# A's results beside B's merge, the weights' pool open over the stages, sums of h in three places, later tiles in the pools of h and T

## The chip, the cores and the metric

The kernel runs on 1 core of one Trainium2 chip. The metric is the device time of one execution in microseconds, as the median of several runs. In the profile PE is the matrix engine (PEld its weight loads), DVE the vector engine, ACT the scalar engine, POOL the GpSimd engine; SP does nothing here but issue DMAs, and its row in the trace is its queue, in which DMAs are issued strictly one after another.

## The reference, cut to what matters

One layer over 1024 tokens of width 1024, all in float32. `h` is the modulated RMSNorm of `x`; one projection of `h` gives the columns of three branches (A attention, B short gated convolution, C conformer convolution) and of three gates.

```python
z = h @ w_in                                   # 1024 x 8704 columns
ya = neighbourhood_attention(q, k, v, kc, vc, rpb) * silu(z[..., A_Z:B_B])
yb = bg * dw_conv(cg * val, w_conv) * silu(gz)
yc = silu(layer_norm(dw_conv(a * sigmoid(g), w31) + b)) * silu(z[..., C_Z:GATES])
ga, gb, gc = split(sigmoid(z[..., GATES:]), 3)
m = ga * (ya @ w_out_a) + gb * (yb @ w_out_b) + gc * (yc @ w_out_c)
out = x + gate * (m @ w_o)
```

## The kernel before

Everything lies transposed: 128 channels on the partitions, tokens along the row. A 128x512 tile is one half of the 1024 tokens of 128 channels. Float32 products are made of three matmuls of the faster fp32r kind: an operand is split into a high part (an ACT cast, `wh`, `ysh`, `lnh`) and a low part (the rest, a subtraction on DVE or POOL, `wl`, `ysl`, `lnl`), and hi x hi, hi x lo and lo x hi are added up in a PSUM bank. `split` and `wsplit` do that.

The stages, with their times in the profiled execution:

1. To 120 us: the modulation of x, its normalisation into `ha0` to `ha7` (high) and `hb0` to `hb7` (low, the list `hlf`), and the first projections.
2. 120 to 565 us: attention of four head pairs (`attend(hp)`), beside it the projections of the next pair (`qkv`, `glu`) and, at the end, eight plain projections (`plain`) that go to memory as `zad` and `zbd`. The results of attention go to memory as `yad`. `plain(6)` and `plain(7)` of the gates are issued behind the last attention's matmuls (`zaps`, `flt`).
3. 570 to 943 us: the other columns in groups of two column tiles (`group`, run through `b_start`, `b_end`, `gate_pair`, and the last two as `last_two`). A group uses seven products instead of eight blocks, with sums of blocks of `h` (tiles `T1` to `T3`, and `T4`) and of weights (`s1` to `s4`). The sums of `h` are made by `h_sums(j)`, j = 0 to 3, on POOL during stage 2 (eight instructions `hsum` each), stored in memory as `td`, and read back by `load_t`. The convolution C runs beside the groups on DVE (`conv_step`). `a_result(i, b)` multiplies A's result by its gate path on POOL (`yain`), splits it (`ysh` on ACT, `ysl` on POOL) and stores both parts in `ysd[1]`; B's results go to `ysd[0]`. Gates go to memory as `gd`.
4. 943 us to the end: three merges, each over 8 column tiles `dm` and two halves `b`, 12 matmuls each (`ops`): B first, then A, then C; the layer norm of C (`norm_steps`) advances beside B and A by a fixed number of steps per half: column sums by matmul (`sums`), the reciprocal root (`rsqrt_mean` on POOL, `diag` on DVE), its spread over the partitions (`rstd`), and the normalised and gated result (`zcin`, `ych`). A merge's PSUM halves are multiplied by the gate (`gs`, loaded from `gd`) on DVE and added into `mt`. At the end, a product with `w_o` (`fin`).

The order in which each engine works is set by the program order and a scheduler that plans it beforehand; on the chip every engine takes its list strictly in order. Between stages 3 and 4 all pools are closed and new ones opened, so a tile of stage 4 waits for the last user of the memory that it lies on.

Of the kernel before, what the change touches and what calls it, by code (L numbers as in the profile page):

```python
# [8 lines left out]
F32 = mybir.dt.float32  # L9
# [33 lines left out]
def tile_hybrid(ctx: ExitStack, tc, x, xT, cx, cond, crow, ng, w_ada, b_ada, wqkv, wz,  # L43
# [5 lines left out]
    hctx = ExitStack()  # L49
    hp_pool = hctx.enter_context(tc.tile_pool(name="hT", bufs=1))  # L50
# [68 lines left out]
    ysd = [[[dram.tile([P, S], F32, name=f"ysd{n}{i}{h}") for h in range(2)] for i in range(4)] for n in range(2)]  # L119
# [10 lines left out]
    def qkv(hp, w=None, cts=None, first=(), psc=None, mid=None):  # L130
# [41 lines left out]
        def context():  # L172
            vc = [a1.tile([P, 2, P], F32R, tag=f"vc{h}", name="vc") for h in range(2)]
# [64 lines left out]
    A_t = cst.tile([P, KT, 2], F32, name="A_t")  # L238
    B_t = cst.tile([P, KT, 2], F32, name="B_t")
# [224 lines left out]
    with tc.tile_pool(name="at", bufs=1, reuse_waits="tile") as at, \  # L464
# [45 lines left out]
        def attend(hp):  # L510
            ya = at.tile([P, 16, 64], F32, tag="ya", name="ya", bufs=1)
            for h in range(2):
# [9 lines left out]
                for cb in range(4):  # L522
# [54 lines left out]
                    dve.tensor_tensor(out=ya[hs, :, cb * 16 : cb * 16 + 16],  # L577
# [36 lines left out]
        for hp in range(4):  # L614
            attend(hp)
            if hp < 3:
                qkv(hp + 1, w1 if hp == 0 else None)
            h_sums(hp)
            if hp < 3:
                glu(hp + 1)  # L620
        for i in range(4):
            plain(ZA + i, zad[i])
# [4 lines left out]

    sctx = ExitStack()
# [22 lines left out]
    T = [[pair(sp.tile([P, 2, 512], F32R, name=f"T{i}_{j}")) for j in range(4)] for i in (1, 2, 3)]  # L651
    T4 = [pair(hlf[1][j]) for j in range(4)]

    def load_t(blocks, i):
        for j in range(4):
            t = s512("traw", "hs", 4)
            nc.sync.dma_start(t, td[i][j])
            split(*blocks[j], t, dve)

    with tc.issue_after(state["py"].ins):  # L660
        for i in (6, 7):
            plain(GT + 2 * KT + i, gd[2 * KT + i], True)
    for i in (1, 0, 2):
        load_t(T[i], i)
    load_t(T4, 3)
# [3 lines left out]
    wq = gctx.enter_context(tc.tile_pool(name="wq", bufs=1, side="right", reuse_waits="tile"))  # L669
# [56 lines left out]
    def group(ct0, ct1, use0, use1, few=pool):  # L726

        raw = []
        for ct in (ct0, ct1):
            r = wq.tile([P, D], F32, tag="wr", name="wr", bufs=3)  # L730
# [34 lines left out]

    def last_two(cts, uses):
# [24 lines left out]
        for n in two:  # L791
# [4 lines left out]
            dve.tensor_tensor(out=x[n], in0=f, in1=x[n], op=ALU.add)  # L796
        s3 = [s_(n, raw[n][0], raw[n][2], ALU.subtract, "s3") for n in two]
# [7 lines left out]
        for n in two:  # L805
# [5 lines left out]
            uses[n][1](0, y[n])  # L811
        s4 = [s_(n, raw[n][1], s2[n], ALU.subtract, "s4") for n in two]
        for n in two:
# [40 lines left out]
    def spill_split(t, n, i, b, eng):  # L854
# [3 lines left out]
        for h, o in enumerate((hi, lo)):  # L858
            nc.sync.dma_start(ysd[n][i][h][:, B512[b]], o.bitcast(F32))

# [341 lines left out]
```

## Time and profile before

| | |
|---|---|
| median of 3 runs | 1205.05 us (1199.15 to 1205.64) |
| the profiled execution | 1200.33 us, of which the span is 1198.5 us |
| mean granted clock of PE in it | 0.964 |
| PE busy | 1126.9 us (94%) |
| DVE, POOL, ACT busy | 850.8, 663.4 and 560.8 us |
| DMA | 167.87 MB, mean 140 GB/s |

All rows of the trace are of the profiled execution, and its 1200.33 us is 4.7 us under the median. A row of the timeline gives start, duration, engine, line, operation, the tile written and the tiles read, and in brackets how long the engine had been idle before it and what released it. A row of the windows gives, per stretch of time, each engine's busy time with its count of instructions, the granted clock of PE (1.00 is full), the share of DMA and the rate. A row of the chains of waits gives the waiting instruction, what released it, the total, the count and the longest.

### The profile page before, as it was taken

What the parts mean: (1) busy time and instruction counts of PE and PEld (TensorE: products, weight loads), DVE (VectorE), ACT (ScalarE), POOL (GpSimd) and SP (SyncE); (2) the same over time, 40 slices, a digit from 0 to 9 for tenths busy, and PEclk for the clock granted to TensorE, in tenths of its full rate; (3) what the DMA queues carried; (4) which work ended last, traced back from release to release, by engine and by line L of the source; (5) the groups of instructions that cost most, each with busy time, mean ns of one, the idle gap of its engine ahead of it and who ended that gap; (6) DMA issues with size and microseconds to landing.
All of it is one profiled execution on the core that took longest, in us unless ns stands there. A gap on an engine that the chain in (4) does not pass through costs nothing.

```text
span 1198.5 us, 16663 instructions
## 1 busy us (share of the span) xinstructions
PE 1126.9 (94%) x5566; PEld 961.0 (80%) x5566; DVE 850.8 (71%) x1495; ACT 560.8 (47%) x1167; POOL 663.4 (55%) x623
## 2 busy tenths in 40 slices
PE   5779699999999999998999999999999798999998
PEld 4678699899899788886788888887877476888887
DVE  7995768788877875657993897896993356679311
ACT  5575358557656688784333332324334335313110
POOL 6675845645745833310887677868888006851110
PEclk7789899999999999999899999999999798999999
DMA  9235242332322313117234434345653694662621
GB/s 354 106 136 180 72 126 84 104 108 85 111 64 77 118 63 121 56 42 236 93 102 142 124 105 149 101 154 173 190 192 132 242 406 153 205 241 88 237 80 53
DMA packets 88151, 167.87 MB, mean 140 GB/s; under 512 B 11008, under 2 KB 39424, under 8 KB 88064
## 3 DMA queue, kind: packets, MB, share of 16 engines
q1 hardware_dynamic: 83456, 164.70, 40.9%
q10 hardware_dynamic: 4608, 2.10, 0.6%
q8 instruction: 44, 0.72, 0.3%
q14 instruction: 43, 0.35, 0.1%
HBM read 120.62 MB, written 46.14 MB: 139 GB/s over the span
## 4 chain that ended last, share of the span: by engine, by line
PE 59%; DVE 17%; DMA 8%; POOL 7%; issue 4%; ACT 3%; SPq 1%; POOLq 0%; DVEq 0%; ACTq 0%
DVE cv L690 4%; PE ops L107 4%; PE ops L109 4%; PE ops L108 4%; PE pp L564 3%; PE zaps L108 3%; PE zaps L107 3%; PE zaps L109 3%; PE ps L109 3%; PE ps L107 3%; PE ps L108 3%; PE fin L109 2%; PE fin L107 2%; PE fin L108 2%; DMA wada<-in_w_ada 2%
## 5 line engine op out<-in xcount | busy, mean ns | idle before, releaser
L90 POOL TENSOR_TENSOR wl<-wr,wh 128x384 fp32r<-128x384 f32 (+2 forms) x93 | 89.6, 969 | 182.2 <-ACT wh L88 156.1
L690 DVE SCALAR_TENSOR_TENSOR cv<-upad,cf_t,cv 128x512 f32<-128x512 f32 x240 | 166.9, 747 | 0.2
L88 ACT CAST wh<-wr 128x384 fp32r<-128x384 f32 (+2 forms) x138 | 61.2, 456 | 113.5 <-DMA wr<-in_wout 46.9
L533 POOL TENSOR_TENSOR bias<-mka,vimg 128x288 f32<-128x288 bf16 (+1 forms) x64 | 59.5, 931 | 87.8 <-DVE mn L547 76.5
L639 POOL TENSOR_TENSOR wl<-s,wh 128x512 fp32r<-128x512 f32 x57 | 79.5, 1409 | 11.1 <-ACT wh L638 6.4
L638 ACT CAST wh<-s 128x512 fp32r<-128x512 f32 x76 | 46.1, 616 | 75.6 <-POOL s L642 64.1
L639 POOL TENSOR_TENSOR wl<-wr,wh 128x512 fp32r<-128x512 f32 x46 | 64.4, 1402 | 22.7 <-ACT wh L638 22.7
L569 DVE TENSOR_TENSOR plo<-pp,ph 128x512 fp32r<-128x512 f32 (+1 forms) x96 | 60.8, 640 | 8.5 <-ACT ph L567 8.0
L714 PE MATMUL ga<-ha,wh 128*128 128x512 f32 x152 | 60.6, 398 | 6.5 <-ACT wh L638 4.7
L564 PE MATMUL pp<-ident,pbuf 128*128 128x128 f32 x352 | 59.1, 273 | 1.6 <-DVE pbuf L553 1.3
L716 PE MATMUL ga<-ha,wl 128*128 128x512 f32 x152 | 60.3, 397 | 0.2 <-POOL wl L639 0.2
L715 PE MATMUL ga<-ha,wh 128*128 128x512 f32 x152 | 60.2, 396 | 0.0
L567 ACT CAST ph<-pp 128x512 fp32r<-128x512 f32 (+1 forms) x96 | 51.7, 547 | 16.8 <-PE pp L564 16.0
L549 ACT ACTIVATE pbuf<-sc,mn 128x256 f32<-128x256 f32 x64 | 30.4, 475 | 60.1 <-DVE mn L547 59.6
L1116 DVE SCALAR_TENSOR_TENSOR o<-fin,gate,xr 128x512 f32<-128x512 f32 x16 | 12.0, 751 | 59.7 <-PE fin L109 59.7
L551 DVE TENSOR_TENSOR mn<-mn 128x1 f32<-128x1 f32 x64 | 17.6, 275 | 47.0 <-ACT pbuf L550 46.7
L109 PE MATMUL fin<-mh,wl 128*128 128x512 f32 x128 | 49.8, 389 | 0.0
L108 PE MATMUL fin<-ml,wh 128*128 128x512 f32 x128 | 49.8, 389 | 0.0
L107 PE MATMUL fin<-mh,wh 128*128 128x512 f32 x128 | 49.7, 389 | 0.0
L564 PEld LDWEIGHTS pp<-ident,pbuf 128*128 128x128 f32 x352 | 42.7, 140 | 7.0 <-DVE pbuf L553 2.6
L90 DVE TENSOR_TENSOR wl<-wr,wh 128x384 fp32r<-128x384 f32 (+2 forms) x45 | 31.6, 705 | 13.9 <-ACT wh L88 13.9
L79 POOL TENSOR_TENSOR ssh<-ssh,half_neg 128x4 f32<-128x4 f32 (+1 forms) x40 | 39.4, 987 | 2.7
(382 smaller groups left out, 3970.3 us busy)
## 6 DMA issues: line engine op xcount, KB each, us to landing
wr<-in_wz SPq DMA_DIRECT2D x36, 512.0 KB, 3.9
gs<-gd SPq DMA_DIRECT2D x24, 512.0 KB, 5.2
wada<-in_w_ada SPq DMA_DIRECT2D x16, 512.0 KB, 8.7
wr<-in_wz SPq DMA_DIRECT2D x36, 192.0 KB, 2.5
cht<-chd SPq DMA_DIRECT2D x24, 256.0 KB, 3.1
gd<-gate SPq DMA_DIRECT2D x22, 256.0 KB, 3.1
vimg<-in_rpbs SPq DMA_DIRECT2D x16, 288.0 KB, 3.0
gd<-c SPq DMA_DIRECT2D x18, 256.0 KB, 3.1
```

The costliest lines, as they stand in the source:

```text
L88: act.copy(hi[:, :n], raw[:, :n])
L90: state["lo"] = lo_eng.tensor_tensor(out=lo[:, :n], in0=raw[:, :n], in1=hi[:, :n].bitcast(F32), op=ALU.subtract)
L107: pe.matmul(ps, ah, bh, start=i == 0, stop=False)
L108: pe.matmul(ps, ah, bl, start=False, stop=False)
L109: pe.matmul(ps, al, bh, start=False, stop=i == n - 1)
L564: pe.transpose(out=pp[:, c * 256 + hf * P : c * 256 + hf * P + P], in_=pts[hf][:, o : o + P], identity=ident)
L569: dve.tensor_tensor(out=plo[:, : m * 256], in0=pp[:, : m * 256], in1=ph[:, : m * 256].bitcast(F32), op=ALU.subtract)
L639: eng.tensor_tensor(out=lo, in0=src, in1=hi.bitcast(F32), op=ALU.subtract)
L690: dve.scalar_tensor_tensor(out=acc[b], in0=src, scalar=cf_t[:, i, j : j + 1], in1=acc[b], op0=ALU.mult, op1=ALU.add)
L714: pe.matmul(ps, wh, bh, start=first and j == 0, stop=False, skip_group_check=True)
L715: pe.matmul(ps, wh, bl, start=False, stop=False, skip_group_check=True)
L716: pe.matmul(ps, wl, bh, start=False, stop=last and j == 3, skip_group_check=True)
```

## The change

Six things are done.

- `h_sums` is called nowhere after the first head pair, with j = 0 after the second, j = 1 after the third, and with 2 and 3 after the fourth.
- The pool of `h` stays open to the end, with waits by tile; `T1` to `T3` lie in a pool `tp` of their own that also stays open. `load_t` loads a sum straight into the place of the low part and splits it there; T1 to T3 are loaded ahead of `plain(6)` and `plain(7)`, T4 behind the first group. A dummy tile fixes where the first tile `cht` lies.
- The first group loads its weights into two tiles of the pool `sp` (`wry`), because the pool of weights is not yet open.
- `a_result` leaves the groups. Beside B's merge, A's results and their gate paths are loaded as whole 128x1024 tiles (`a_load`), multiplied on POOL (`yz`) and split in place (`ya`), with no way through memory.
- The weights' pool `wq` stays open, so the merges load their weights in pairs (`w_raw`, `wro`) and split them 512 wide; the first two pairs, B's results (`yb`), and C's convolution (`cvin`) are loaded and prepared during `last_two`, into the tiles of T and `h` that are no longer read. The last product's weights go the same way (`wrf`).
- `norm_steps` begins two tiles of B's merge later and takes three steps per half beside B and two beside A; `rstd` is 2 matmuls of 512 columns instead of 8 of 128; `big` has 8 buffers instead of 10.

On POOL, at the start of attention (in these rows `hsum` is a sum of h, `vc`, `vs` and `ssh` belong to the context's and the latents' keys and values, `bias` to the first scores). Before:

```order
L598 TENSOR_TENSOR hsum_2457<-ha0_175 128x512
L598 TENSOR_TENSOR hsum_2459<-hb0_463 128x512
L598 TENSOR_TENSOR hsum_2463<-hb4_682 128x512
L200 TENSOR_TENSOR vc_1228<-rawc_1280,vc_1228 128x64
L200 TENSOR_TENSOR vc_1229<-rawc_1280,vc_1229 128x64
L598 TENSOR_TENSOR hsum_2469<-ha4_179 128x512
L200 TENSOR_TENSOR vc_1228<-rawc_1295,vc_1228 128x64
L533 TENSOR_TENSOR bias_1415<-mka_1366,vimg_1411 128x288
L200 TENSOR_TENSOR vc_1229<-rawc_1295,vc_1229 128x64
L533 TENSOR_TENSOR bias_1432<-mka_1366,vimg_1413 128x288
L533 TENSOR_TENSOR bias_1488<-mka_1366,vimg_1411 128x384
```

After:

```order
L202 TENSOR_TENSOR vc_1221<-rawc_1273,vc_1221 128x64
L202 TENSOR_TENSOR vc_1222<-rawc_1273,vc_1222 128x64
L202 TENSOR_TENSOR vc_1221<-rawc_1288,vc_1221 128x64
L536 TENSOR_TENSOR bias_1408<-mka_1359,vimg_1404 128x288
L202 TENSOR_TENSOR vc_1222<-rawc_1288,vc_1222 128x64
L536 TENSOR_TENSOR bias_1425<-mka_1359,vimg_1406 128x288
L536 TENSOR_TENSOR bias_1481<-mka_1359,vimg_1404 128x384
L77 TENSOR_SCALAR ssh_1277<-ssh_1277 128x2
L510 TENSOR_TENSOR vs_1394<-vb_1303,vs_1394 128x8x64
L510 TENSOR_TENSOR vs_1711<-vb_1303,vs_1711 128x8x64
```

The sums of h are gone from between the key's and the bias's instructions. On ACT, from the loads of T to the first group's weights (`wh` of `wr` or `wry`; `s` are the group's sums of weights). Before:

```order
L638 CAST T3_0_6434<-traw_6618 128x512
L638 CAST T3_1_6435<-traw_6622 128x512
L638 CAST T3_2_6436<-traw_6626 128x512
L638 CAST T3_3_6437<-traw_6630 128x512
L589 ACTIVATE flt_6583<-zaps_6558 128x512
L638 CAST hb0_463<-traw_6634 128x512
L638 CAST hb1_517<-traw_6638 128x512
L638 CAST wh_6674<-wr_6665 128x512
L638 CAST hb2_571<-traw_6642 128x512
L638 CAST hb3_625<-traw_6646 128x512
L638 CAST wh_6695<-s2_6670 128x512
```

After:

```order
L645 CAST T3_6431<-T3_6431 128x512
L645 CAST T3_6432<-T3_6432 128x512
L645 CAST T3_6433<-T3_6433 128x512
L592 ACTIVATE flt_6587<-zaps_6562 128x512
L592 ACTIVATE flt_6615<-zaps_6590 128x512
L645 CAST wh_6642<-wry_6633 128x512
L645 CAST wh_6663<-s2_6638 128x512
L645 CAST wh_6682<-s1_6637 128x512
L645 CAST wh_6702<-s3_6639 128x512
L645 CAST wh_6734<-wry_6633 128x512
L645 CAST wh_6754<-s4_6640 128x512
```

The casts of T3 now stand ahead of both last sigmoids (`flt`), those of T4 (`hb0` to `hb3`) behind the first group's; the first cast of weights is the one right behind the last sigmoid. On PE, at the end of the last group (`ge`) and the start of the merges. Before:

```order
L714 MATMUL ge_9971<-hb7_724,wh_9972 128x512
L715 MATMUL ge_9971<-hb7_724,wh_9972 128x512
L716 MATMUL ge_9971<-hb7_724,wl_9973 128x512
L1006 MATMUL sums_10085<-lnh_10086,onesr_10028 128x512
L1007 MATMUL sums_10085<-lnl_10087,onesr_10028 128x512
L1006 MATMUL sums_10085<-lnh_10104,onesr_10028 128x512
```

After:

```order
L723 MATMUL ge_9898<-hb7_716,wh_9899 128x512
L724 MATMUL ge_9898<-hb7_716,wl_9900 128x512
L106 MATMUL ops_9942<-yb_9675,wh_9832 128x512
L107 MATMUL ops_9942<-yb_9677,wh_9832 128x512
L108 MATMUL ops_9942<-yb_9675,wl_9833 128x512
```

B's merge (`ops`) follows the last product directly; the first `sums` comes after 60 matmuls of it. On ACT that `sums` waits for the cast `lnh` of `cvin`, which stands after: 

```order
L645 CAST wh_10225<-wro_10160 128x512
L911 ACTIVATE gate_9856<-ga_9767 128x512
L645 CAST wh_10320<-wro_10317 128x512
L911 ACTIVATE gate_9875<-ga_9792 128x512
L645 CAST wh_10376<-wro_10317 128x512
L645 CAST ya_9956<-yz_10041 128x512
L911 ACTIVATE px_9629<-px_9629 128x512
L645 CAST ya_9956<-yz_10076 128x512
L645 CAST ya_9974<-yz_10120 128x512
L645 CAST ya_9974<-yz_10153 128x512
L645 CAST wh_10428<-wro_10425 128x512
L645 CAST lnh_10046<-cvin_9817 128x512
```

Before, A's results came split from memory, so ACT had no cast `ya` at all. On SP, the gates of B's first tiles (`gs`) stand after:

```order
L912 DMA gd18_143<-gate_9856 128x512
L818 DMA wro_10540<-in_wout 128x512 x2
L801 DMA ya_10014<-zad3_104 128x1024
L912 DMA gd20_145<-gate_9875 128x512
L912 DMA gd20_145<-px_9629 128x512
L818 DMA wro_10655<-in_wout 128x512 x2
L1008 DMA gs_9939<-gd8_133 128x1024
L1008 DMA gs_9978<-gd9_134 128x1024
```

They come behind the weights of later tiles (`wro`), which wait for a free buffer.

The diff, cut to its core:

```diff
@@ attention and what is beside it
-            h_sums(hp)
             if hp < 3:
+                for j in ((), (0,), (1,))[hp]:
+                    h_sums(j)
                 glu(hp + 1)
+        for j in (2, 3):
+            h_sums(j)
...
-            t = s512("traw", "hs", 4)
-            nc.sync.dma_start(t, td[i][j])
-            split(*blocks[j], t, dve)
-
+            hi, lo = blocks[j]
+            nc.sync.dma_start(lo.bitcast(F32), td[i][j])
+            split(hi, lo, lo.bitcast(F32), dve)
+
+    for i in (1, 0, 2):
+        load_t(T[i], i)
     with tc.issue_after(state["py"].ins):
         for i in (6, 7):
             plain(GT + 2 * KT + i, gd[2 * KT + i], True)
-    for i in (1, 0, 2):
-        load_t(T[i], i)
-    load_t(T4, 3)
...
-    wq = gctx.enter_context(tc.tile_pool(name="wq", bufs=1, side="right", reuse_waits="tile"))
+    wq = ctx.enter_context(tc.tile_pool(name="wq", bufs=1, side="right", reuse_waits="tile"))
@@ group
+            if early:
+                r = sp.tile([P, S], F32, tag="y", name="wry", bufs=2)
+            else:
+                r = wq.tile([P, D], F32, tag="wr", name="wr", bufs=3)
@@ new, between group and last_two
+    homes = {"mt": [f"ha{i}" for i in range(KT)], "cv": [f"hb{i}" for i in range(4)], "ya0": [f"hb{i}" for i in range(4, 8)],
+             "ya1": ["T3"], "yb": ["T1"] * 4 + ["T2"] * 4}
...
+    def a_load(i):
+        hi, lo = (of(("ya1", "ya0")[i // 2], "ya") for _ in range(2))
+        nc.sync.dma_start(hi.bitcast(F32), yad[i])
+        nc.sync.dma_start(lo.bitcast(F32), zad[i])
+        return hi, lo
+
+    def a_result(hi, lo):
+        for b in range(2):
+            sl = B512[b]
+            t = tmp("yz")
+            pool.tensor_tensor(out=t, in0=hi[:, sl].bitcast(F32), in1=lo[:, sl].bitcast(F32), op=ALU.mult)
+            split(hi[:, sl], lo[:, sl], t, pool)
+            yield
...
+    def w_raw(br, dm):
+        r = wq.tile([P, D], F32, tag="wr", name="wro", bufs=3)
+        for n in range(2):
+            nc.sync.dma_start(r[:, B512[n]], wout[br, dm + n])
+        for n in range(2):
+            wnext[br, dm + n] = r[:, B512[n]]
...
@@ last_two
+        yb_s.extend(loaded_y(i, "yb") for i in range(4))
...
+        for i in range(4):
+            t = of("cv", "cvin", F32)
+            nc.sync.dma_start(t, cvd[i])
+            cv.append(t)
+        w_merge(1, 0)
+        w_merge(1, 1)
@@ the groups
-            pool.tensor_tensor(out=y, in0=z, in1=y, op=ALU.mult)
-            spill_split(y, 1, i, b, pool)
...
+        if i == 0:
+            load_t(T4, 3)
...
-        for _ in range(1 + (i in (0, 2, 4))):
-            a_result(*halves.pop(0))
@@ the merges
-            w = load_w(wout[br, dm], 4, dve if dm % 2 else pool)
+            w = w_merge(br, dm)
...
             rstd.append(ps)
...
     def beside_b(dm, b):
-        if (dm, b) == (4, 0):
-            ya_s.extend(loaded_y(1, i, "ya") for i in range(4))
+        if dm < 2:
+            a_parts.append(a_load(2 * dm + b))
+        else:
+            next(asteps, None)
+        for _ in range(3 if dm > 1 else 0):
+            next(steps, None)
```

115 lines of the change are left out of this document (67 added, 48 removed).

## The prediction

> **What bounds the kernel now.** First the page's span, the engines' busy time and the 40 slices, to find the engine that is never long idle.
>
> ```profile
> span 1198.5 us, 16663 instructions
> PE 1126.9 (94%) x5566; PEld 961.0 (80%) x5566; DVE 850.8 (71%) x1495; ACT 560.8 (47%) x1167; POOL 663.4 (55%) x623
> PE   5779699999999999998999999999999798999998
> PEclk7789899999999999999899999999999798999999
> ```
>
> PE is the bound: nearly all slices read 9. What can be won lies in the dips: the first 100 us (which the change does not touch), the fifth slice (120 to 150 us), the 19th (540 to 570) and the 32nd and 33rd (930 to 990). Both PE's busy share and its granted clock sag there. Next the chains of waits of PE, which name the gaps.
>
> ```profile
> PE sl L541 <- DVE ks L505: 8.4, 1, 8.4
> PE sums L1006 <- ACT lnh L638: 7.7, 2, 7.2
> PE ga L714 <- ACT wh L638: 4.7, 1, 4.7
> PE rstd L1052 <- DVE diag L1051: 4.2, 1, 4.2
> PE ga L714 <- ACT p L738: 1.0, 1, 1.0
> PE pskc L194 <- DVE tmc L221: 1.3, 1, 1.3
> ```
>
> Waits show only the gaps; a low clock after a gap costs as well. So the windows are read by the count of matmuls. Columns: stretch, its length, then busy time and count of PE, PEld, DVE, ACT, POOL, then clock, DMA share, GB/s.
>
> ```profile
> 125.00:150.00 25.00, 15.07 (x72) 14.27 (x70) 18.74 (x11) 7.73 (x20) 24.48 (x28) 0.80 0.21 67
> 550.00:575.00 25.00, 20.11 (x79) 15.74 (x78) 22.68 (x35) 12.50 (x22) 4.55 (x4) 0.89 0.80 267
> 825.00:850.00 25.00, 23.96 (x106) 19.54 (x105) 14.71 (x19) 8.99 (x17) 19.69 (x15) 1.00 0.68 222
> 875.00:900.00 25.00, 23.19 (x101) 18.36 (x99) 23.92 (x38) 11.04 (x20) 23.67 (x19) 1.00 0.48 160
> 925.00:950.00 25.00, 17.96 (x80) 14.54 (x78) 6.44 (x10) 6.11 (x11) 1.40 (x2) 0.90 0.43 146
> 950.00:975.00 25.00, 22.06 (x67) 14.89 (x68) 15.24 (x24) 14.05 (x27) 1.58 (x2) 0.76 1.03 407
> 975.00:1000.00 25.00, 20.73 (x84) 16.53 (x83) 14.37 (x41) 2.44 (x5) 2.82 (x3) 0.86 0.79 310
> 1025.00:1050.00 25.00, 25.00 (x112) 20.71 (x111) 17.34 (x24) 5.50 (x12) 19.13 (x15) 1.00 0.72 229
> ```
>
> The last row is a full stretch: 112 matmuls of 512 columns in 25 us, 0.223 us each. Against it 925 to 950 is short of 32 (7.1 us), 950 to 975 of 45 (10.0). In 975 to 1000 some 16 of the 84 records are the small `rstd` ones (12 in the row of part 4), which I estimate at 11 full ones, so 33 are missing (7.4). The start of the merges thus loses 24.5 us, far more than its 7.7 + 4.2 of waits. It is the largest prize.
>
> **Part 1, sums of h leave the start of attention.** POOL's list and DVE's there, from the timeline:
>
> ```profile
> 128.72 7.42 DVE L501 TENSOR_TENSOR qlz<-qT,qd 64x1024 fp32r<-64x1024 f32 x1
> 130.49 2.50 POOL L598 TENSOR_TENSOR hsum<-hb 128x512 f32<-128x512 f32 x2
> 136.36 1.73 DVE L501 TENSOR_TENSOR qlz<-qT,qd 64x1024 fp32r<-64x1024 f32 x1
> 136.96 2.57 POOL L533 TENSOR_TENSOR bias<-mka,vimg 128x288 f32<-128x288 bf16 x2
> ```
>
> The first `qlz` takes 7.42 us while POOL runs memsets and sums of h; its twin beside `bias` takes 1.73. If the first falls to that, `ks` is 5.7 us earlier and the 8.4 us gap shrinks to 2.7. The 1.3 us at `pskc` waits for a POOL operation behind two more `hsum` (2.5 us) and goes too: 7.0 us. Of the low clock behind the gap (0.80 in the stretch) I count no gain. Ends: 2, if only the sums queued ahead on POOL matter and `qlz` is slow for another reason; 9, if the clock recovers sooner as well.
>
> The trace has a second gap of that size:
>
> ```profile
> 540.62 0.38 PE L573 MATMUL py<-ph,vs 128*128 128x256 f32 x1 [1.93 <-DVE ya L577]
> 543.00:546.00 3.00, 3.00 (x9) 2.37 (x9) 0.06 (x1) 0.00 (x0) 0.00 (x0) 0.57 0.71 239
> ```
>
> A gap of 1.93 us was followed by a clock of 0.57, so a remaining 2.7 us will be too, and that is why I keep the clock's loss. The Trainium skill (TensorE: Matmul & The Clock Gate, Part 1) says that the clock is halved only after an idle window of about 3.4 us; by it the remaining gap would leave the clock alone, and this part would be worth an estimated 2 us more, 9 in all. The row contradicts it, and I go by the row.
>
> The sums are not dropped: 8 of them move behind the fourth head pair, where 8 stand already. 8 x 1.25 us is 10 us of POOL's list around 415 to 430, which had room: 17.1 of 25 us busy, with PE idle for 1.9.
>
> ```profile
> 400.00:425.00 25.00, 23.07 (x126) 19.21 (x126) 19.01 (x39) 15.40 (x32) 17.10 (x16) 1.00 0.37 118
> ```
>
> I take 1 us lost, between 0 and 5.7 (one `qlz`-like collision).
>
> **Part 2, the start of the groups.** PE's 4.7 us gap:
>
> ```profile
> 564.32 0.90 SPq L731 DMA_DIRECT2D wr<-in_wz  x2
> 565.63 0.60 ACT L589 ACTIVATE flt<-zaps 128x512 f32<-128x512 f32 x1
> 569.62 0.62 ACT L638 CAST wh<-wr 128x512 fp32r<-128x512 f32 x1 [1.95 <-DMA wr<-in_wz]
> 570.29 0.79 PE L714 MATMUL ga<-ha,wh 128*128 128x512 f32 x1 [4.71 <-ACT wh L638]
> 573.00:576.00 3.00, 3.00 (x8) 2.35 (x8) 2.55 (x3) 2.22 (x5) 3.00 (x3) 0.50 0.15 57
> ```
>
> The weights are asked for at 564.3, behind the loads of T, and land at 569.6. Now 12 loads of T leave before `plain(6)`, and the weights follow its first store, some 14 us earlier. They are not the last to come any more: the cast `wh` stands on ACT right behind the last sigmoid, which ends at 566.2. So `wh` is ready at 566.9 instead of 570.3 (3.4 us), PE idles 1.3 us, and the six microseconds at half clock, which cost 2.9, should not follow, since the 1.0 us gap behind `p` in 825 to 850 left the clock at 1.00 (above). Sum 6; ends 3 (the clock drops anyway) and 7. T's new loads overlap the `plain` weights' loads; DMA was 0.80 busy in this stretch, and moving 3 MB earlier relieves it.
>
> **Part 3, A's results leave the groups.** By groups of instructions (busy, mean ns, idle before and its releaser):
>
> ```profile
> L866 POOL TENSOR_TENSOR yain<-zain,yain 128x512 f32<-128x512 f32 x8 | 11.0, 1373 | 9.5 <-DMA zain<-zad 9.0 <-DVE cv L690 0.5
> L639 POOL TENSOR_TENSOR ysl<-yain,ysh 128x512 fp32r<-128x512 f32 x8 | 10.8, 1347 | 0.7 <-ACT ysh L638 0.7
> L744 DVE TENSOR_TENSOR u<-gf,p 128x512 f32<-128x512 f32 x17 | 11.6, 684 | 5.8 <-POOL yain L866 5.4 <-ACT p L738 0.3
> ```
>
> POOL was 23.7 of 25 us busy in 875 to 900, and stood 9.0 us waiting for `zain`; 21.8 us of its work, 8 ACT casts and 32 transfers of 256 KB go. The row of `u` shows DVE waiting 5.4 us for `yain`, and PE behind it. The two windows above lose 6 + 11 matmuls (3.8 us); with an estimate for the stretch between them I take 5 us, between 0 (the gaps are the convolution's on DVE, 23.9 of 25 busy) and 6.6. Beside B's merge the 16 POOL operations at 1.36 us, 22 us, fall into a stretch where POOL does 1.4 to 2.8 us in 25: free. The 8 loads of 512 KB replace 16 of 256 KB.
>
> **Part 4, the start of the merges.** The gap before `sums` and the `rstd` in the timeline, and the page's DMA issues of the gates (count, size, median us from issue to landing):
>
> ```profile
> 949.52 0.62 ACT L638 CAST lnh<-cvin 128x512 fp32r<-128x512 f32 x1 [3.68 <-DMA cvin<-cvd]
> 950.19 0.79 PE L1006 MATMUL sums<-lnh,onesr 128*128 128x512 f32 x1 [7.23 <-ACT lnh L638]
> 993.18 3.54 PE L1052 MATMUL rstd<-diag,ones 128*128 128x128 f32 x12 [4.19 <-DVE diag L1051]
> ```
>
> ```profile
> gs<-gd SPq DMA_DIRECT2D x24, 512.0 KB, 5.2
> ```
>
> Let T0 be the end of the last product (942.9 before). B's results, `cvin` and two pairs of weights are there by then, so 60 matmuls of B's merge run at once: to T0 + 13.4 (60 x 0.223). Then PE meets `sums`, whose `lnh` stands on ACT behind `wh_10225`. That cast needs a place in the ring of 8 weight tiles, free when the second column tile is done: 48 matmuls, T0 + 10.7. Behind it are 10 ACT operations to the end of `lnh`'s predecessor and `lnh` itself at 0.62: T0 + 17.5. So PE idles 4.1 us there and runs about 12 matmuls at half clock (12 x 0.21 = 2.5). The gates: `gs` stands on SP behind a pair of weights whose buffer falls free when POOL and DVE have split an earlier pair, about T0 + 16; PE's 6 banks are full at 6 x 12 matmuls plus this gap, about T0 + 22. A transfer takes 5.2 us, so it lands at 21 to 22: just in time, and I count 2 us of stumbling. `rstd` now has 3 + 4 extra steps between its parts, some 39 matmuls (8.7 us) against the 4.2 us it waited and an estimated 2 us more for making two whole `diag` first: no wait. Loss after: 4.1 + 2.5 + 2 = 8.6 against 24.5, so 16 won. Ends 8 (gates late by another transfer and a half, 8 us) and 20 (ACT faster than counted).
>
> What comes next is POOL in A's merge: mt adds, 16 norm products, splits of weights.
>
> ```profile
> L980 POOL TENSOR_TENSOR mt<-mt,gs 128x512 f32<-128x512 f32 x16 | 21.7, 1359 | 15.4 <-DVE gs L979 8.1 <-PE ops L108 5.6 <-DMA wr<-in_wout 1.8
> L1066 POOL TENSOR_TENSOR zcin<-zcin,cvin 128x512 f32<-128x512 f32 x8 | 11.8, 1479 | 0.1
> L1064 POOL TENSOR_TENSOR cvin<-cvin,lsg 128x512 f32<-128x512 f32 x8 | 10.7, 1338 | 0.7 <-ACT cvin L1063 0.7
> ```
>
> 18 x 1.36 (14 `mt`, 4 splits taken alike) + 8 x 1.48 + 8 x 1.34 is 47 us from `rstd` to the last `zcin`, which C's merge wants about 50 us after `rstd`. It fits with 3 us to spare; at 1.5 us each throughout it would be 51, 1 us late. Weights 512 wide save casts on ACT, which is not the bound: nothing. The smaller `big` ring and the new last product's loads: nothing, PE had no gap after 1000 and the loads run ahead.
>
> **Sum.** 7 - 1 + 6 + 5 + 16 = 33 us off the profiled 1200.3: 1167. The runs' median lies 4.7 above that execution, so I forecast 1171.
>
> **Rivals.** (a) The merges keep most of their loss. SP's queue issues the gates only when a weight buffer falls free; if that is 8 to 12 us later than counted, PE's banks stay full that long, and part 4 is worth 4 to 8 instead of 16. For it: the DMA share was 1.03 in 950 to 975. Against: much of that load is now before T0. Time 1171 + 10 = 1181. (b) The sums of h do not matter: `qlz` stays at 7.42, because memsets ran beside it too and stay. Then part 1 gives 1.3 and the moved sums cost 1 or more: 1171 + 6 = 1177, or 1181 with a collision. (c) Slower. DVE's operations with two operands stick beside POOL as `qlz` did, 5.7 us each, now in the merges, where POOL has a list without a pause. The gain of 33 is eaten by six such collisions on PE's path, and at eight the time is 1171 + 8 x 5.7 = 1217. Against it stands the row 1025 to 1050, where POOL (19.1) and DVE (17.3) are both full and PE lacks nothing. The Trainium skill (GPSIMD Engine Reference, Key points) has such a rule: GpSimd shares its SBUF interfaces with DVE, in contention with DVE's two-input instructions; the trace has it in one row of two. (d) The tiles' waits tie the early weights to something late, and the start of the groups does not move: 1171 + 6 = 1177.
>
> **How the numbers follow.** Forecast 0.60; (a) 0.19; (b) 0.09; (d) 0.08; (c) 0.04. The low end is all upper ends together, 9 + 7 + 6.6 + 20 = 42.6, taken from the faster runs: 1157. The high end takes (a) and (b) or (d) together: 1171 + 10 + 6 + 3 = 1190. Half a per cent, 6 us, is what a measurement of this kernel tells from no change: faster needs 1199 or less, which all cases but (c) and a pile of the others give: 0.93. Same 0.03, slower 0.04.
>
> **What would show it.** Right: `qlz` near 1.7 us and a gap of under 3 us before the first `sl`; the first `ga` within 1.5 us of the last `zaps`, at full clock; windows of 112 matmuls from 825 to T0; `ops` directly behind the last `ge`, one gap of about 4 us before `sums`, none before `rstd`. Wrong: a gap of PE behind `gs` in B's first tiles, `qlz` still at 7, or a wait for `ych` at the start of C's merge.

## The result, and the profile after

The changed kernel took 1165.18 us (median of 4 runs, 1162.96 to 1165.82); the kernel before took 1205.35 (4 runs, 1199.15 to 1208.35). The ratio is 0.967, with a 95% interval of 0.963 to 0.971. The forecast was 1171, in a range of 1157 to 1190. The profiled execution took 1165.39 us, with a span of 1163.4 us, 35.1 less than before. The medians lie 40 us apart, because the profiled execution of the kernel before was 5 us under its median and that of the changed kernel lies at its own; all that follows explains the 35. The page of the changed kernel:

```profile
span 1163.4 us, 16409 instructions
PE 1112.9 (96%) x5554; PEld 953.3 (82%) x5554; DVE 841.9 (72%) x1479; ACT 556.6 (48%) x1135; POOL 666.7 (57%) x607
PE   6779899999999999999999999999999999999998
PEclk6689999999999999999999999999999999999999
```

The dips of PE at 540 to 570 and 930 to 990 us are gone from the slices, and the one at the start of attention is smaller. POOL, DVE and ACT work as long as before, within some 1%: what was saved is waits of PE, and matmuls at a low clock (PE's busy time fell by 14.0 us with only 12 matmuls less). From the chains of waits of PE, those at the places that the change touches:

```profile
PE pskc L196 <- DVE tmc L223: 2.7, 1, 2.7
...
PE ops L107 <- DVE ycl L646: 2.2, 1, 2.2
...
PE fin L106 <- ACT mh L645: 1.4, 1, 1.4
PE sl L544 <- DVE ks L508: 1.3, 1, 1.3
...
PE ga L722 <- ACT wh L645: 1.2, 1, 1.2
PE ops L106 <- DVE px L894: 0.8, 1, 0.8
```

The 8.4 us at `sl`, 7.7 at `sums`, 4.7 at `ga` and 4.2 at `rstd` of before have become 1.3, nothing, 1.2 and nothing. The wait at `pskc` was 1.3 before; those at `ycl` (C's merge) and `mh` (the last product) are new. The windows of the changed kernel, with the columns as before:

```profile
125.00:150.00 25.00, 20.99 (x109) 20.09 (x108) 15.22 (x19) 11.28 (x26) 20.32 (x27) 0.86 0.21 60
200.00:225.00 25.00, 21.50 (x115) 17.15 (x114) 21.26 (x39) 15.27 (x37) 16.27 (x15) 1.00 0.30 96
400.00:425.00 25.00, 21.35 (x115) 17.15 (x114) 20.55 (x36) 12.76 (x30) 22.20 (x20) 1.00 0.36 118
550.00:575.00 25.00, 23.81 (x105) 19.15 (x104) 20.95 (x28) 13.36 (x25) 13.63 (x10) 1.00 0.79 304
875.00:900.00 25.00, 25.00 (x112) 20.71 (x111) 11.06 (x17) 11.63 (x21) 22.57 (x18) 1.00 0.52 187
925.00:950.00 25.00, 24.22 (x107) 19.74 (x106) 15.80 (x18) 13.00 (x24) 25.00 (x17) 1.00 1.02 401
950.00:975.00 25.00, 25.00 (x112) 20.69 (x111) 19.56 (x42) 11.55 (x20) 2.27 (x3) 1.00 0.36 116
1025.00:1050.00 25.00, 22.68 (x100) 18.11 (x99) 21.56 (x26) 5.19 (x9) 16.87 (x10) 1.00 0.74 245
```

The stretch around the start of the merges (925 to 975) is full but for 5 matmuls, where it lacked 77 before. Two stretches got worse: 200 to 225 (PE 21.5 busy, and 23.89 before, in the row below), 400 to 425 (21.35, and 23.07 before); and one where nothing was lost before is now short by 12 matmuls, 1025 to 1050, the start of C's merge. The kernel before:

```profile
200.00:225.00 25.00, 23.89 (x131) 19.54 (x130) 22.38 (x42) 15.81 (x37) 17.60 (x16) 1.00 0.26 83
```

For each stage I added up by how much each matmul's distance to the next exceeds the usual one of its shape, the median in the trace (0.227 us for 512 columns). This sum, the ledger in what follows, counts waits and low clock together. PE loses 115.1 us in this way in the trace of before and 81.7 in that of the changed kernel, some 47 of them in each before 125 us, which the change does not touch:

| stage | before | after | won | forecast |
|---|---|---|---|---|
| start of attention (125 to 175) | 15.5 | 9.6 | 5.9 | 7 |
| second and fourth head pair (200 to 225, 400 to 450) | 6.0 | 12.0 | -6.0 | -1 |
| start of the groups (525 to 575) | 11.8 | 4.1 | 7.7 | 6 |
| groups (575 to 925) | 7.7 | 0 | 7.7 | 5 |
| start of the merges (925 to 1000) | 25.1 | 1.9 | 23.2 | 16 |
| C's merge and last product (from 1000) | 0.1 | 4.6 | -4.5 | 0 |

The sum is 34, with 33 forecast: two terms were too small by 2 to 3 us, one by 7, and two losses of 5 us were not seen. That it comes out within 1 us is luck, since these errors cancel. Each figure is from one execution, and some hold a low clock that comes by chance (1.6 us of the 7.7 at the start of the groups, as the account below shows).

### The profile page after: what moved, and what is told of

It is laid out like the page before. It is cut to its first block, busy times and chain, and to the rows that moved or that the text cites. A ratio compares the mean times of both kernels' runs of the same rounds, so it can differ in the third digit from the quotient of the medians.

```text
span 1163.4 us, 16409 instructions
## 1 busy us (share of the span) xinstructions
PE 1112.9 (96%) x5554; PEld 953.3 (82%) x5554; DVE 841.9 (72%) x1479; ACT 556.6 (48%) x1135; POOL 666.7 (57%) x607
## 5 line engine op out<-in xcount | busy, mean ns | idle before, releaser
L536 POOL TENSOR_TENSOR bias<-mka,vimg 128x288 f32<-128x288 bf16 (+1 forms) x64 | 56.6, 884 | 87.3 <-DVE mn L550 79.2
L89 POOL TENSOR_TENSOR wl<-wr,wh 128x384 fp32r<-128x384 f32 (+1 forms) x57 | 56.8, 1001 | 54.1 <-ACT wh L87 42.4
L646 POOL TENSOR_TENSOR wl<-wr,wh 128x512 fp32r<-128x512 f32 x44 | 60.5, 1375 | 4.2 <-ACT wh L645 4.2
L570 ACT CAST ph<-pp 128x512 fp32r<-128x512 f32 (+1 forms) x96 | 51.5, 548 | 15.5 <-PE pp L567 14.9
L646 POOL TENSOR_TENSOR wl<-wrf,wh 128x512 fp32r<-128x512 f32 x8 | 12.6, 1574 | 65.2 <-ACT wh L645 56.8
L750 POOL TENSOR_TENSOR s<-wr 128x512 f32<-128x512 f32 x16 | 23.2, 1448 | 38.9 <-DMA wr<-in_wz 38.8
```

The source lines that it names most:

```text
L89: state["lo"] = lo_eng.tensor_tensor(out=lo[:, :n], in0=raw[:, :n], in1=hi[:, :n].bitcast(F32), op=ALU.subtract)
L536: pool.tensor_tensor(out=bv, in0=mv, in1=iv, op=ALU.subtract)
L646: eng.tensor_tensor(out=lo, in0=src, in1=hi.bitcast(F32), op=ALU.subtract)
```

## Experiments

**The sums of h back to their old places in the changed kernel (sums_old), and their new places alone in the kernel before (before_sums).**

```diff
# sums_old: from after;  before_sums: from before, the other way round
-            if hp < 3:
-                for j in ((), (0,), (1,))[hp]:
-                    h_sums(j)
-                glu(hp + 1)
-        for j in (2, 3):
-            h_sums(j)
+            h_sums(hp)
+            if hp < 3:
+                glu(hp + 1)
```

> The changed kernel, with the sums of h put back to where they were (one call behind each of the four head pairs). Theory 1 (ledger): the move won about 6 us at the start of attention and gave as much back behind the second and the fourth head pair, where matmuls now come more sparsely (10 windows short by 2.8 and 3.2 us more than before), so this kernel takes the time of the changed one within 3 us, 1162 to 1168, with the first qlz back at 7.4 us and a gap of about 8 us before the first sl. Theory 2 (the prediction): the move is worth 6 us net, so this takes 1170 to 1173.

> The kernel before, with only the sums of h moved as the change moves them. Theory 1 (ledger): no difference beyond 3 us, ratio 0.998 to 1.002, because the 6 us won at the start of attention are lost again behind the second and fourth head pair. Theory 2 (the prediction): 6 us faster, ratio 0.995.

sums_old took 1169.3 us (1167.5 to 1170.8), ratio 0.9715 (0.9691 to 0.9739): between the two theories, its span 3.6 us longer than the changed kernel's. By the same ledger it loses 7.6 us more at the start of attention and 6.1 less behind the second and fourth head pair; 1.6 more come where the last head pair ends, from a low clock after a gap of 1.93 us that both kernels have. So the whole move is worth some 2 to 4 us, not 6, and the intervals of the two ratios overlap. before_sums took 1203.48, ratio 1.0005 (0.9988 to 1.0021): nothing, as theory 1 said. By the ledger 7.3 us are won at the start of attention and 6.1 lost again behind the second and fourth head pair. What is left goes into another wait:

```profile
PE ga L717 <- ACT wh L641: 8.9, 1, 8.9
```

The gap ahead of the first group is 8.9 us instead of 4.7. PE arrives 2.6 us earlier (1.6 of them because the clock does not fall behind the gap of 1.93 us this time), and the weights do not: they are asked for at 563.9 us (564.3 before), and the first cast of them begins at 571.2 (569.6 before). In the old kernel a gain ahead of that point turns into waiting at it; that part 2 of the change is what lets part 1 count is argued, not shown.

**Eight adds, or sixteen memsets, on POOL at the start of attention (sums_dup, sums_memset).**

```diff
+            if hp == 0:                       # sums_dup
+                for o in range(2):
+                    for k in range(4):
+                        t = tmp("hsum")
+                        pool.tensor_tensor(out=t, in0=hlf[o][k][:, 0].bitcast(F32), in1=hlf[o][k][:, 1].bitcast(F32), op=ALU.add)
+            if hp == 0:                       # sums_memset
+                for o in range(8):
+                    t = tmp("hsum")
+                    for k in range(2):
+                        pool.memset(t, 0.0)
```

> The changed kernel, with 8 additional adds of two 128x512 tiles on POOL where the sums of the first head pair stood, their results unused and nothing stored. Theory 1 (contention): DVE's first qlz, which reads two operands, takes about 7 us again beside POOL's adds, and PE's gap before the first sl is about 7 us instead of 1.3. Theory 2 (the transfers or the low clock made qlz slow, not the adds): qlz stays at 1.2 to 1.7 us and the gap under 4 us, though POOL's list is 10 us longer.

> As the run with the 8 adds, but with 16 memsets of 128x512 on POOL in their place: POOL's queue is as long, but it reads no operand. Theory 1 (contention through operands read): qlz stays at 1.2 to 1.7 us, and the gap before the first sl under 4 us. Theory 2 (anything that POOL does there delays DVE, or the length of its queue): qlz at 7 us or the gap at 6 us and more, as with the adds.

The timeline of the run with adds, then of the run with memsets:

```profile
129.07 7.42 DVE L504 TENSOR_TENSOR qlz<-qT,qd 64x1024 fp32r<-64x1024 f32 x1
129.60 3.75 POOL L625 TENSOR_TENSOR hsum<-ha 128x512 f32<-128x512 f32 x3
133.87 1.25 POOL L625 TENSOR_TENSOR hsum<-ha 128x512 f32<-128x512 f32 x1
141.12 0.58 PE L544 MATMUL sl<-ks,qd 128*128 128x288 f32 x1 [8.43 <-DVE ks L508]
```

```profile
128.93 1.22 DVE L504 TENSOR_TENSOR qlz<-qT,qd 64x1024 fp32r<-64x1024 f32 x1
129.44 1.46 POOL L625 MEMSET hsum<- 128x512 f32 x3
133.07 0.37 PE L544 MATMUL sl<-ks,qd 128*128 128x288 f32 x1 [0.53 <-DVE ks L508]
144.97 0.48 PE L196 MATMUL pskc<-ident,tmc 128*128 128x128 f32 x1 [7.19 <-DVE tmc L223]
```

Beside adds that read two operands on POOL, DVE's `qlz` takes 7.42 us, six times as long as beside memsets, while POOL's adds keep their 1.25. Theory 1 holds for `qlz` and for the first `sl`, and it is the rule that the Trainium skill (GPSIMD Engine Reference, Key points) states without a number. But the length of POOL's queue has a price of its own: with the memsets, PE waits 7.19 us at `pskc` instead, behind the later operations of POOL that `tmc` needs. Each was run once: 1174.4 and 1170.4 us.

**A's results back in the groups (a_groups).**

```diff
@@ in the loop over the last five groups
         conv_step(1)
+        for _ in range(1 + (i in (0, 2, 4))):
+            a_early(*halves.pop(0))      # load, multiply (POOL), split (ACT and POOL), store in ysa
@@ beside B's merge
-        nc.sync.dma_start(hi.bitcast(F32), yad[i])
-        nc.sync.dma_start(lo.bitcast(F32), zad[i])
+        nc.sync.dma_start(hi.bitcast(F32), ysa[i][0])
+        nc.sync.dma_start(lo.bitcast(F32), ysa[i][1])
...                                          # and a_result no longer multiplies and splits
```

> The changed kernel, with A's results multiplied, split and stored in the groups again, and loaded split beside B's merge. Theory 1 (ledger): the stretch from 575 to 900 us lost 7.7 us of matmul time before and none after, all of it by A's results on POOL, so this kernel is 6 to 8 us slower than the changed one, 1171 to 1173, with gaps of about 1 us in the last five groups. Theory 2: the gaps came from the convolution on DVE and from the weights' loads, which the change eased elsewhere; then it is within 2 us of the changed one. Prediction: 5 us.

It took 1175.0 us (1172.6 to 1177.7), ratio 0.9767 (0.975 to 0.9785), some 10 us more than the changed kernel; the profiled execution is the fastest of its four, with a span 7.4 us longer. The windows from 800 to 925, all full in the changed kernel, lose 9.2 us by the ledger. Three gaps of PE there, from the timeline:

```profile
869.27 0.50 PE L723 MATMUL ga<-ha,wh 128*128 128x512 f32 x1 [1.10 <-DVE u L756]
891.59 0.50 PE L723 MATMUL gd<-hb,wh 128*128 128x512 f32 x1 [1.36 <-DVE c L729]
916.33 0.50 PE L723 MATMUL gd<-hb,wh 128*128 128x512 f32 x1 [2.90 <-DVE pz L729]
```

Theory 1, and a little more than it asked: with A's results in the groups the gaps are back, and without them there are none. The run moves POOL's products, ACT's casts and the transfers together; that POOL is what holds PE up is shown for the first gap, where DVE's `u` had waited 2.41 us for `yain`, and not for the others. The lower end that the prediction kept for this term (0, if the gaps were the convolution's on DVE) is excluded.

**The two halves of part 2 apart (t_late, w_late).**

```diff
@@ t_late: T1 to T3 are loaded behind plain(6) and plain(7) again
-    for i in (1, 0, 2):
-        load_t(T[i], i)
     with tc.issue_after(state["py"].ins):
         ...
+    for i in (1, 0, 2):
+        load_t(T[i], i)
@@ w_late: the first group's weights come from the pool of weights
-        run(CG + i, BV + i, meet, meet, dve, i == 0)
+        run(CG + i, BV + i, meet, meet, dve)
```

> The changed kernel, with the loads of T1 to T3 behind the last two plain projections again; the first group's weights still go to the other pool. Theory 1: the early weights alone are not enough, since T's loads and casts on ACT stand ahead of the first cast of weights; a gap of 3 us or more before the first ga, low clock after it, 5 to 8 us slower than 1165. Theory 2: the weights were the last to come, and T's place does not matter: within 2 us of 1165.

> The changed kernel, with the first group's weights in the pool of weights, which opens only when the last plain projections are done; T's loads stay early. Theory 1: the weights are asked for at the end of the plain projections; a gap of 3 to 5 us before the first ga, low clock after, 4 to 8 us slower than 1165. Theory 2: without T's loads ahead of them in the queue the weights come in time: within 2 us.

t_late took 1165.8 us (ratio 0.969, 0.9676 to 0.9703), w_late 1175.3 (0.9773, 0.9759 to 0.9786). SP's queue in t_late, and PE's first group in w_late:

```profile
540.69 3.17 SPq L665 DMA_DIRECT2D T<-td  x5
```

```profile
567.96 0.79 PE L722 MATMUL ga<-ha,wh 128*128 128x512 f32 x1 [3.82 <-ACT wh L645]
```

The early weights are worth about 10 us of time (6.3 of them in 550 to 575, gap and low clock; 2.2 in a later group). The place of T's loads in the program is worth nothing, but not because T may come late: five of the twelve loads still left at 540.7, ahead of the first store of `plain`. The scheduler lets a load rise to where its memory is free, wherever it is written.

**The preparation of the merges (no_ahead, w2_pool, homes_new).**

```diff
@@ no_ahead: the three pieces leave last_two and stand ahead of the merges
-        yb_s.extend(loaded_y(i, "yb") for i in range(4))
-        for i in range(4): ...                   # cvin <- cvd
-        w_merge(1, 0)
-        w_merge(1, 1)
@@ w2_pool: no_ahead, and
-    wq = ctx.enter_context(...)
+    wq = gctx.enter_context(...)                 # closes with the groups
+    w2 = ctx.enter_context(tc.tile_pool(name="w2", bufs=9, side="right", reuse_waits="tile"))
-            w = w_merge(br, dm)
+            w = load_w(wout[br, dm], 4, dve if dm % 2 else pool)
@@ homes_new: no_ahead, and
+    hctx.close()                                 # the pools of h and T
+    pools = {n: (ctx.enter_context(tc.tile_pool(name=n, bufs=1, reuse_waits="tile")), k) for n, k in kinds}
```

> The changed kernel, but B's results, C's convolution and the first weights of the merges are loaded and split only behind the last two groups in program order, as before. Theory 1: the gain at the start of the merges (25.1 us lost before, 1.9 after) is this preparation ahead; without it PE has a gap of 4 us or more before the merges, the clock drops, and the time is 8 to 20 us longer than 1165. Theory 2: the tiles' own waits (pools that stay open) are what lets the work start early, wherever it is written; then the loads rise by themselves and the time stays within 3 us of 1165.

> The changed kernel with the preparation of the merges written behind the last groups (which alone cost nothing), and in addition the weights' pool closed there and a new one opened for the merges and the last product, with weights loaded and split 384 and 128 wide as before. B's results and C's convolution still go to the tiles of T and h. Theory 1: the open weights' pool carries a good part of the 23 us won at the start of the merges; the first weights come several us after the last product, PE has a gap of 3 us or more and a low clock after it, 5 to 12 us slower than 1165. Theory 2: B's results and the convolution's were the late ones, and the weights are no bottleneck: within 3 us of 1165.

> The changed kernel with the preparation written behind the last groups, and the tiles for B's, A's and C's results and the sums taken from new pools that open when the pools of h and T have closed, as before. The weights' pool stays open. Theory 1: these tiles' memory is read by the last products, so B's results and the convolution land several us after them; a gap of 5 us or more, low clock, 8 to 18 us slower than 1165. Theory 2: the weights are what was late, and this is within 3 us of 1165.

no_ahead took 1164.96 us (ratio 0.9692, 0.9676 to 0.9708): nothing lost, theory 2. B's results still left from 893.9 us on, 34 us ahead of the merges. w2_pool took 1175.1 (0.9754, 0.9728 to 0.978) and homes_new 1175.1 (0.9757, 0.9734 to 0.9779): each takes some 8 to 10 us away (8 between the spans, 10 between the medians). w2_pool also splits the weights 384 and 128 wide again, which was not tried apart from the pool, and the two were not undone together. In w2_pool, ACT and PE at the start of the merges:

```profile
932.22 0.71 ACT L87 CAST wh<-wr 128x384 fp32r<-128x384 f32 x2 [1.98 <-DMA wr<-in_wout]
932.78 0.80 PE L106 MATMUL ops<-yb,wh 128*128 128x512 f32 x1 [4.97 <-ACT wh L87]
```

The first weights are late, as theory 1 of that run said (7.1 us lost in 925 to 950, and 1.1 in the changed kernel); the rest of its loss comes at the last product (5.2 us in 1075 to 1100, 1.7 in the changed kernel), with a clock of 0.93. In homes_new the start of the merges is not late; PE stops in small steps at the column sums, and then the clock falls:

```profile
947.28 0.50 PE L1048 MATMUL sums<-lnl,onesr 128*128 128x512 f32 x1 [0.95 <-DVE lnl L647]
949.76 0.77 PE L1047 MATMUL sums<-lnh,onesr 128*128 128x512 f32 x1 [1.75 <-DVE cvin L1072]
```

```profile
950.00:958.00 8.00, 6.65 (x14) 4.31 (x15) 8.00 (x11) 4.05 (x7) 4.54 (x3) 0.50 0.43 146
```

Here the convolution's results arrive after the products, not before (`cvin` was asked for from 924.1 us, and at 911.6 in the changed kernel). The size was as theory 1 expected, the place not: not one gap of 5 us ahead of B's merge, but steps within it.

**Two versions meant to be better (better, better2).**

```diff
@@ both: the sums of h behind the plain projections of A's gate path
         for i in range(4):
             plain(ZA + i, zad[i])
+            h_sums(i)
@@ better: crs four steps later, half of the adds into mt in A's merge on DVE
+        for _ in range(4):
+            yield
         act.activation(crs, cr, AF.Sigmoid)
-                    (pool if br == 0 else dve).tensor_tensor(out=mt...
+                    (pool if br == 0 and b == 0 else dve).tensor_tensor(out=mt...
@@ better2: crs on DVE in its place, and half of the adds of C's merge on POOL
-        pool.tensor_tensor(out=crs, in0=crs, in1=cr, op=ALU.mult)
+        dve.tensor_tensor(out=crs, in0=crs, in1=cr, op=ALU.mult)
+                    (pool if b == (br == 2) and dm < 7 else dve).tensor_tensor(out=mt...
```

In better2, too, half of the adds of A's merge are on DVE.

> The changed kernel with three small edits: the sums of h behind the four plain projections of A's gate path, none between the head pairs; the product for the last gate (crs, 2.9 us on POOL) four steps later in C's merge; and half of the adds into mt in A's merge on DVE. Theory 1: PE's 2.9 and 1.7 us lost at the start of C's merge and of the last product go, and 3 to 5 of the 6 us lost beside the second and fourth head pair, so 1156 to 1160. Theory 2: the losses come back elsewhere (DVE late with ycl, or POOL's adds holding DVE in the last head pair): within 2 us of 1165.

> As the run with three small edits, but the product crs is made on DVE where it stood instead of later, and half of the adds into mt in C's merge are on POOL. Theory 1: the 5.7 us that the run with three edits lost before the last product (DVE had the eight reductions of the last gate four steps later, among the adds and splits of mt) go, and the start of C's merge stays free: 1154 to 1158. Theory 2: DVE was already full at the end of C's merge in the changed kernel (1.7 us lost there), and the wait for mh stays at 2 us or more: 1158 to 1162.

better took 1161.9 us (1160.5 to 1162.2), ratio 0.964 (0.9616 to 0.9663); better2 1162.95, ratio 0.9668 (0.9655 to 0.9682). Both beat the kernel before; against the changed kernel's 0.967 (0.963 to 0.971) the intervals overlap, so neither is shown to be faster than it. better lies between its two theories (1156 to 1160, and 1163 to 1167). In their traces, as planned, PE loses nothing more at the start of C's merge (2.9 us in the changed kernel) and 8 us less at 200 to 225 and 400 to 425 together; but 2 come back at 475 to 500, and 5.7 (better) and 7.3 (better2) at the last product:

```profile
1071.73 1.22 PE L106 MATMUL fin<-mh,wh 128*128 128x512 f32 x2 [3.10 <-ACT mh L642]
```

That is from better. The forecast of 1154 to 1158 for better2 failed: DVE was no longer full there (6.9 of 10 us), yet PE still waited for `mh`, whose chain now goes through an add on POOL of 1.7 us instead of 0.68 on DVE. On this path POOL's room was no help, because the add took longer there; the run does not try it without that add.

## Why the prediction came out, term by term

**The start of attention (7 forecast, 5.9 measured).** `qlz` fell to 1.23 us and the first gap to 1.3, better than forecast, and sums_dup and sums_memset show the cause that the prediction named. But the 1.3 us at `pskc` were not won; they became 2.7, since `tmc` still waits for POOL. In this execution that gap was again followed by a low clock:

```profile
140.94 0.48 PE L196 MATMUL pskc<-ident,tmc 128*128 128x128 f32 x1 [2.66 <-DVE tmc L223]
...
144.00:147.00 3.00, 3.00 (x12) 3.00 (x11) 1.69 (x4) 2.24 (x4) 2.01 (x3) 0.50 0.01 2
```

So the 3.4 us that the Trainium skill names (TensorE: Matmul & The Clock Gate, Part 1) are not the least gap that can halve the clock, and the prediction was right to keep the loss. But its reason, that a gap of 1.93 us will be followed by a low clock and a longer one too, does not hold, and that the loss came here is luck. The same gap of 1.93 us stands in the changed kernel, at full clock behind it; and in t_late, whose program is the same up to there, the gap at `pskc` is as long and the clock stays at 1.00:

```profile
540.61 0.38 PE L576 MATMUL py<-ph,vs 128*128 128x256 f32 x1 [1.93 <-DVE ya L580]
543.00:546.00 3.00, 3.00 (x15) 2.49 (x14) 0.05 (x1) 0.00 (x0) 0.00 (x0) 1.00 0.54 189
```

```profile
141.21 0.33 PE L196 MATMUL pskc<-ident,tmc 128*128 128x128 f32 x1 [2.65 <-DVE tmc L223]
144.00:147.00 3.00, 3.00 (x19) 3.00 (x18) 1.67 (x5) 2.19 (x4) 2.46 (x3) 1.00 0.07 22
```

Of the 14 traces of this document 8 have a low clock behind the gap at `py` and 6 have not. Ten have a gap of 2.65 us at `pskc`: with a low clock behind it (six) the stretch from 125 to 175 us loses 8.0 to 9.7 us, without (four) 6.5 to 7.1.

**The sums moved to other head pairs (1 forecast, 6.0 measured).** The step that failed is the sentence that POOL had room there. It had, 17.1 of 25 us; but the cost lies on DVE, whose operations take longer beside POOL's: between 204 and 208 us, beside the sums, `pbuf` took 1.26 us, and 0.40 in the kernel before at 204.7, where POOL was idle. Behind the second head pair, which the prediction left out, the kernel before has eight sums as well; in the changed kernel POOL's order around them is another, and the longest gap there (1.62 us at 204.2) follows an addition `mn` of DVE that took 1.21 us beside POOL's `vs`, and 0.14 before. What in the new order makes up the rest was not tried apart. The prediction had a price of this size in its bound (one collision, 5.7 us) and took nearly the other end. In sums_old both stretches go back to what they were before (2.6 and 3.3 us).

**The start of the groups (6 forecast, 7.7 measured).** Of the 7.7 us, 1.6 are the low clock behind the gap at `py`, which the trace of before has and that of the changed kernel has not; without them the term is 6.1. The first cast of weights stands right behind the last sigmoid, PE's gap is 1.2 us and the clock stays at 1.00, as worked out (1.3 forecast):

```profile
564.01 0.60 ACT L592 ACTIVATE flt<-zaps 128x512 f32<-128x512 f32 x1 [4.84 <-PE zaps L108]
564.50 0.61 ACT L645 CAST wh<-wry 128x512 fp32r<-128x512 f32 x1
565.17 0.50 PE L722 MATMUL ga<-ha,wh 128*128 128x512 f32 x1 [1.19 <-ACT wh L645]
```

The prediction's reason was half right: w_late shows that it is the weights, and t_late that moving T's loads in the program adds nothing.

**A's results (5 forecast, 7.7 by the ledger, 7 to 10 by a_groups).** Mechanism right, too small, and beyond the upper end of 6.6: A's results in the groups and not the convolution alone made the gaps. Beside B's merge they were not quite free of effect either: POOL is busy all of 925 to 950, and DVE's `lnl` there has a median of 1.2 us, where it had 0.69 before. PE does not wait for it.

**The start of the merges (16 forecast, 23.2 measured).** This is the term that was mis-sized most, beyond its upper end of 20. The 4.1 us gap before `sums` and its low clock did not come. The step that failed is that `wh_10225` waits for the second column tile of B's merge. In the trace it runs at 923.8, 4 us ahead of the merges, behind a product of the last group; `ops` begins at 928.2, and ACT:

```profile
933.73 0.62 ACT L645 CAST wh<-wro 128x512 fp32r<-128x512 f32 x1 [2.95 <-PE ops L107]
934.26 1.66 ACT L645 CAST lnh<-cvin 128x512 fp32r<-128x512 f32 x3
```

The cast that waits is a later one, and it waits for the first column tile only; the first `lnh` is ready 6.7 us into the merge, and `sums` needs it at 941.9, 14 us into it. The gates were issued at 931.8, 4 us into it and not 16, so rival (a) had no ground, nor had the 2 us of stumbling. w2_pool and homes_new show that doing without the open weights' pool (with its wider splits) or without the tiles of h and T costs 8 to 10 us each, and no_ahead that the code's place inside `last_two` carries nothing.

**C's merge (0 forecast, -4.5 measured).** The prediction priced POOL's list in A's merge at 47 us of 50 and left out the product `crs`:

```profile
1028.33 2.85 POOL L1130 TENSOR_TENSOR crs<-crs,cr 128x1024 f32<-128x1024 f32 x1
1031.14 1.29 POOL L646 TENSOR_TENSOR wl<-wro,wh 128x512 fp32r<-128x512 f32 x1
1032.39 2.27 POOL L1119 TENSOR_TENSOR zcin<-zcin,cvin 128x512 f32<-128x512 f32 x1
...
1039.18 0.50 PE L107 MATMUL ops<-ycl,wh 128*128 128x512 f32 x1 [2.15 <-DVE ycl L646]
```

Its 2.85 us use up the 3 that the prediction had to spare. DVE has a part in the 2.15 us too: `ych` is ready at 1035.3, and `ycl` begins 2.1 us later, behind the gate's reduction of `crs` and two operations of the merge, and then takes 1.75 us beside POOL's adds, where the shortest such subtraction in the kernel before took 0.68:

```profile
1037.38 1.75 DVE L646 TENSOR_TENSOR ycl<-zcin,ych 128x512 fp32r<-128x512 f32 x1
```

In better, with `crs` later and half of the adds elsewhere, this wait is gone, and also in better2, with `crs` on DVE; which of the edits did it was not tried apart.

Of the rivals, (b) and (d) are refuted by the gaps at `sl` and `ga`. The mechanism of (c) exists: `qlz` in sums_dup, `lnl` in the merges. In the merges of the changed kernel it reached PE's path only at `ycl`, by some 1 us of that operation. Of the six rows of the table only the start of attention lies within the ends that the prediction gave it (the start of the groups does too, without its 1.6 us), so the sum is better than its parts. Its median also carried over the 4.7 us by which the profiled execution lay under the median of before (1167 + 4.7 is 1172, where it has 1171); the changed kernel has no such distance, which is most of the 6 us by which the forecast missed. Why the kernel before varies more, no trace shows.

## What to carry to other kernels

Rank a change's parts by the lost time of the bounding engine per stage (missing matmuls, low clock included), not by the waits alone: the 14 us of waits at the merges stood for 25 lost. A gain ahead of a transfer that comes no earlier is turned into a longer wait for it, so free the later wait first. Pools that stay open with waits by tile let loads rise by themselves; moving the code as well added nothing here. Before a loss at low clock is put to a cause, look whether the same gap in another execution has it too. When work is moved to an engine with room, ask whom its operands hold up and what the operation costs there, and count every instruction on that engine's list up to the deadline.

## What the hardware showed unexpectedly

One DVE operation on two operands of 64x1024 took 1.22 us beside POOL's memsets, 1.73 beside POOL's subtractions with a bf16 operand (`bias`), and 7.42 beside POOL's adds of two float32 operands. These were not slowed (1.25 us), but a later add of sums_dup took 2.26 us, beside DVE's `ks`. DVE's addition `mn` of one element per partition took 0.14 us in the kernel before (202.7) and 1.21 in the changed one (202.6), beside POOL's `vs`.

Whether a short gap halves PE's clock depends on when it comes. In each of the 14 traces all changes of the granted clock lie whole steps of 3.41 us apart, from the first to the last. The gap of 1.93 us at `py` was followed by half clock in the 8 traces in which at least 1.88 us of it lay within one such step, and by full clock in the 6 in which at most 1.70 did. For the gap of 2.65 us at `pskc`, half clock in 6 traces and full in 4, the part within one step does not separate the two, so what else counts is open. Single gaps of about 1.2 us left the clock at 1.00 wherever they stood alone; in homes_new half clock for 10 us began in the third of three gaps of 0.38, 0.95 and 1.75 us within 5 us.
